# Two projections of a DiT block with 512 instead of 256 weight columns per matmul

## The chip, the cores and the metric

The kernel runs on one core of one Trainium2 chip. The metric is the device time of one execution in microseconds (us). A core has TensorE (PE: matmuls into PSUM), VectorE (DVE), ScalarE (ACT), GpSimd (POOL) and SyncE (SP, which here issues every DMA). Each engine works through its own list of instructions in order and waits on semaphores for the others.

## What is computed

One layer of a backbone for diffusion, on 1024 tokens with 1024 features, all in float32: a modulated RMSNorm, one input projection, two groups of heads side by side, an output projection, and a gated MLP with a 3x3 convolution. The part that matters here, cut down:

```python
def token_mixer(h, w_in, ...):
    z = h @ w_in
    zq, zf_f, zf_b, zi, zg, zu = jnp.split(z, ...)        # 512 columns each
    ...                                                   # q, k, v: forward and backward gated scans
    o = rms_norm(o_f + flip(o_b), g_norm) * jax.nn.silu(heads(zg))
    uf = zu.reshape(B, L, 4, 128)
    y_four = jnp.fft.fft2(uf, axes=(1, 3), norm='ortho').real
    return jnp.concatenate([o, y_four], axis=-1)
```

## The kernel before, in words

Matmuls are done in three products: a float32 operand is split into a high part `hi` (rounded to fp32r) and a low part `lo`, and `mm3` adds hi*hi, hi*lo and lo*hi into one PSUM block. A weight page is a tile of 128 x 1024. `wload` loads it raw into one of two buffers `wr`, ScalarE casts it to `hi` (L62), and VectorE subtracts to get `lo` (L63). By default `hi` and `lo` go into the pools `wh` and `wl`, which have two buffers each; the pool `pg` has 33 pages of the same size for everything else (the normed activations `hT` take 16 of them).

The program goes: `start` (norm, projection of `zi`), then four heads in turn (`head_gemm` does their projections with features on the partitions, `hgrn` the chunked scans on VectorE, ScalarE and TensorE), then `mod_part(0)`, `(2)`, `(1)` (modulation vectors: VectorE sums over weights that stream in, L219 and L221, TensorE transposes, L224), `fnet_proj`, `fnet`, `gate_proj`, `gate`, `mod_part(3)`, `out_proj`, and `ffn`. In `hgrn`, the scores stand at L74 (psm), then transposes (L545), products with v (L74), a chain of states on VectorE (L553) and the output products, which ScalarE evacuates at L564.

`fnet_proj` and `gate_proj` are the two projections with tokens on the partitions. Both call `proj_nat`: a slice of 128 tokens is the stationary operand, weight columns move. Before, it goes through two pieces of 256 columns; each piece has two pages (each with four blocks of 128 rows, 256 columns wide), used for all eight token slices, so the four pages of a projection pass through `wh` and `wl` two at a time. A block `psg` of PSUM holds four token slices. `fnet_proj` evacuates into U[0..3] (L596), `gate_proj` through a Silu into four tiles `zg` (L676).

`fnet` does the DFT over positions: VectorE adds and subtracts the U tiles (butterflies, L606 to L621), then for each of four channel groups TensorE multiplies with DFT tables, ScalarE evacuates (L643), TensorE multiplies again, VectorE combines (L662, L663), ScalarE casts the result (L666) and VectorE makes its low part (L667). `gate` scales the heads' outputs (L688), transposes them (L694) and splits them (L696, L697) for `out_proj`.

The order of instructions on each engine is not written out. A scheduler takes the instructions by their place in the program as far as their operands and a free buffer in their pool are there; `wload` has a higher priority from the first head on (`self.ahead`). So work that stands later in the program fills gaps of work that stands earlier, if a buffer for it is free.

Of the kernel before, what the change touches and what calls it, by code (L numbers as in the profile page):

```python
# [34 lines left out]
class Kern:  # L35
# [533 lines left out]
                                     accum_out=self.ssq[:, h * NT + n:h * NT + n + 1])  # L569


    def proj_nat(self, src, evac):

        for piece in range(2):
            ws = [self.wload(src[piece, i]) for i in range(2)]
            for half in range(2):
                pt = self.pst("g")
                for i in range(4):
                    n = 4 * half + i
                    t = slice(i * P, (i + 1) * P)  # L580
                    steps = []
                    for kt in range(NK):
                        q = slice((kt % 4) * 256, (kt % 4 + 1) * 256)
                        wh, wl = ws[kt // 4]
                        hi, lo = self.hT[kt][half]
                        steps.append(((hi[:, t], lo[:, t]), [(wh[:, q], wl[:, q])]))
                    self.mm3([pt[:, i * 256:(i + 1) * 256]], steps)
                evac(piece, half, pt)

    def fnet_proj(self):  # L590
        self.U = [self.pg(F32, "zt") for _ in range(4)]

        def evac(piece, half, pt):
            for j in range(2):
                u = self.U[2 * half + j].rearrange("p (n c) -> p n c", n=2)
                self.nc.scalar.copy(u[:, :, piece * 256:(piece + 1) * 256],  # L596
                                    pt[:, j * 512:(j + 1) * 512].rearrange("p (n c) -> p n c", n=2))
        self.proj_nat(self.I["wzu"], evac)

    def fnet(self):  # L600
        nc, V = self.nc, self.nc.vector
        U = self.U
        C = math.sqrt(0.5)
        s01, s23, d01, d23 = (self.pg() for _ in range(4))
        for o, a, b, op in ((s01, U[0], U[2], ADD), (s23, U[1], U[3], ADD), (d01, U[0], U[2], SUB), (d23, U[1], U[3], SUB)):
            V.tensor_tensor(o, a, b, op=op)  # L606
        lo, hi = slice(0, 512), slice(512, 1024)
        e02, o13, p02, p13 = (self.pg() for _ in range(4))
        V.tensor_tensor(e02, s01, s23, op=ADD)
        V.tensor_tensor(o13[:, lo], s01[:, lo], s23[:, lo], op=SUB)  # L610
        V.tensor_tensor(o13[:, hi], s23[:, hi], s01[:, hi], op=SUB)
        g04 = self.pg()
        V.tensor_tensor(g04[:, lo], e02[:, lo], e02[:, hi], op=ADD)
        V.tensor_tensor(g04[:, hi], e02[:, lo], e02[:, hi], op=SUB)
        V.tensor_tensor(p02[:, lo], d01[:, hi], d23[:, hi], op=SUB)
        V.tensor_tensor(p02[:, hi], d01[:, hi], d23[:, hi], op=ADD)
        g1, g3 = p13, self.pg()
# [1 line left out]
        V.scalar_tensor_tensor(g1[:, hi], p02[:, hi], -C, d23[:, lo], op0=MUL, op1=SUB)  # L619
        V.scalar_tensor_tensor(g3[:, lo], p02[:, lo], -C, d01[:, lo], op0=MUL, op1=ADD)  # L620
        V.scalar_tensor_tensor(g3[:, hi], p02[:, hi], -C, d23[:, lo], op0=MUL, op1=ADD)  # L621
        G = [(g04[:, lo], None), (g1[:, lo], g1[:, hi]), (o13[:, lo], o13[:, hi]), (g3[:, lo], g3[:, hi]), (g04[:, hi], None)]
        tw = [self.pg() for _ in range(3)]
        for i in range(3):
# [44 lines left out]


    def gate_proj(self):
        self.zg = {}

        def evac(piece, half, pt):
            z = self.zg[piece, half] = self.pg(F32, "zt")
            self.nc.scalar.activation(z, pt, AF.Silu)  # L676
        self.proj_nat(self.I["wzg"], evac)

    def gate(self):
        nc, V = self.nc, self.nc.vector  # L680
        r = self.rsqrt_mean(self.ssq, 32, 1.0 / P, "ro")
        gn = self.vec[:, V_HG:V_HG + 1]
        for h in range(NH):
            o = self.o[h]
            for n in range(NT):
                t = slice(n * P, (n + 1) * P)
                z = self.zg[h // 2, n // 4][:, (n % 4) * 256 + (h % 2) * P:(n % 4) * 256 + (h % 2 + 1) * P]
                V.scalar_tensor_tensor(o[:, t], o[:, t], r[:, h * NT + n:h * NT + n + 1], z, op0=MUL, op1=MUL)  # L688
            yh, yl = self.pg(F32R), self.pg(F32R)
            for half in range(2):  # L690
                pt = self.pst("m")
                for i in range(4):
                    n = 4 * half + i
                    nc.tensor.transpose(pt[:, i * P:(i + 1) * P], o[:, n * P:(n + 1) * P], self.ident)  # L694
                s = slice(half * 512, (half + 1) * 512)
                nc.scalar.activation(yh[:, s], pt, AF.Copy, scale=gn)  # L696
                V.scalar_tensor_tensor(yl[:, s], pt, gn, yh[:, s].bitcast(F32), op0=MUL, op1=SUB)  # L697
            self.y[h] = (yh, yl)
# [554 lines left out]
def lay_out(x, c, ctx, c_ctx, w_mod, b_mod, norm1, norm2, w_in, lb_fwd, lb_bwd,  # L1253
            hgrn_norm, w_out, w_up, w_dw, b_dw, w_down, norm_f):
    A = np.ascontiguousarray
    w_mod, w_in, w_out, w_up, w_down = w_mod[0], w_in[0], w_out[0], w_up[0], w_down[0]
    col = lambda v: np.asarray(v).reshape(-1, P).T
    vec = np.concatenate([
        col(b_mod[0]), col(norm1[0]), col(norm2[0]), col(norm_f), col(hgrn_norm[0]),
        col(lb_fwd), col(lb_bwd), col(b_dw[0]),  # L1260
        w_dw[0].reshape(9, NF, P).transpose(2, 1, 0).reshape(P, NF * 9),
        col(c[0]), col(c_ctx)], axis=1)
    assert vec.shape == (P, NV)
    rows = lambda w: w.reshape(NK, P, -1)
    win = rows(w_in)
    ctile = lambda i: win[:, :, i * P:(i + 1) * P].transpose(1, 0, 2).reshape(P, 1024)
    nat = lambda a: win[:, :, a:a + 512].reshape(2, 4, P, 2, 256).transpose(3, 0, 2, 1, 4).reshape(2, 2, P, 1024)
    out = {
        "xT": x[0].T.reshape(NK, P, L),
        "ctxT": ctx[0].T.reshape(2, 4, P, LC).transpose(0, 2, 1, 3).reshape(2, P, 1024),  # L1270
        "vec": vec,
        "wm1": w_mod[:, :2048].reshape(2, 4, P, 2, 8, P).transpose(4, 0, 2, 1, 3, 5).reshape(8, 2, P, 1024),
        "wm2": w_mod[:, 2048:].reshape(NK, P, 4, 1024).transpose(2, 0, 1, 3),
        "wT": np.stack([ctile(4 + i) for i in range(8)] + [ctile(i) for i in range(4)]),
        "wzi": win[:, :, 1536:2048].reshape(4, 2, P, 512).transpose(0, 2, 1, 3).reshape(4, P, 1024),
        "wzg": nat(2048),
        "wzu": nat(2560),
        "wo": rows(w_out).reshape(NK, P, NK, P).transpose(2, 1, 0, 3).reshape(NK, P, 1024),
        "wup": rows(w_up).reshape(NK, P, 2, NF, P).transpose(3, 2, 1, 0, 4).reshape(NF, 2, P, 1024),
        "wd": w_down.reshape(NF, P, D),  # L1280
    }
    out = {k: A(np.asarray(a, dtype=np.asarray(a).dtype)) for k, a in out.items()}
    out.update(shape_constants())
    return out
# [16 lines left out]
```

## Time and profile before

| | |
|---|---|
| time, median of 3 runs | 1234.57 us (1233.62 to 1239.16) |
| the profiled execution: its time, its span | 1235.95 us, 1234.2 us |
| TensorE busy | 1191.5 us, 97% of the span |
| VectorE, ScalarE, GpSimd busy | 913.7 us (74%), 559.3 us (45%), 201.7 us (16%) |
| DMA | 146.23 MB, mean 118 GB/s |
| TensorE's mean granted clock | 0.987 |

Times inside the execution are counted from the start of the span. TensorE's busy time is made of instructions that overlap in a pipeline, with modelled ends, so a busy share near 100% doesn't mean that it works at its peak. The granted clock is a share of full speed: 1.00 is 2.4 GHz and 0.50 is 1.2 GHz. In a chain of waits each piece is the work that the next one waited for.

### The profile page before, as it was taken

What the parts mean: (1) busy time and instruction counts of PE and PEld (TensorE: products, weight loads), DVE (VectorE), ACT (ScalarE), POOL (GpSimd) and SP (SyncE); (2) the same over time, 40 slices, a digit from 0 to 9 for tenths busy, and PEclk for the clock granted to TensorE, in tenths of its full rate; (3) what the DMA queues carried; (4) which work ended last, traced back from release to release, by engine and by line L of the source; (5) the groups of instructions that cost most, each with busy time, mean ns of one, the idle gap of its engine ahead of it and who ended that gap; (6) DMA issues with size and microseconds to landing.
All of it is one profiled execution on the core that took longest, in us unless ns stands there. A gap on an engine that the chain in (4) does not pass through costs nothing.

```text
span 1234.2 us, 15757 instructions
## 1 busy us (share of the span) xinstructions
PE 1191.5 (97%) x6120; PEld 996.5 (81%) x6120; DVE 913.7 (74%) x1173; ACT 559.3 (45%) x804; POOL 201.7 (16%) x124
## 2 busy tenths in 40 slices
PE   7999999999999999999989999999999999999997
PEld 4688888888998888888868888888888887887876
DVE  5761758585877457577989897888888888997683
ACT  5634545454431424364544444444354433335551
POOL 0000000000000000001336455364463400000000
PEclk9999999999999999999989999999999999999998
DMA  8631101010256037453122322222212438635642
GB/s 327 234 121 38 39 18 35 18 35 18 86 162 205 10 120 263 156 187 103 34 77 77 112 94 78 89 90 86 86 69 94 145 111 304 244 112 185 221 157 99
DMA packets 57867, 146.23 MB, mean 118 GB/s; under 512 B 5568, under 2 KB 5824, under 8 KB 57792
## 3 DMA queue, kind: packets, MB, share of 16 engines
q1 hardware_dynamic: 57792, 145.22, 34.1%
q8 instruction: 48, 0.79, 0.3%
q14 instruction: 27, 0.22, 0.1%
HBM read 125.27 MB, written 19.92 MB: 118 GB/s over the span
## 4 chain that ended last, share of the span: by engine, by line
PE 63%; DVE 14%; ACT 9%; DMA 8%; issue 5%; SPq 0%; POOL 0%; DVEq 0%; ACTq 0%; POOLq 0%
PE psm L859 27%; PE psm L74 16%; PE psg L74 14%; PE psm L1036 3%; DMA wr<-in_wd_dram 2%; DVE cv L930 2%; DVE wl L63 2%; DMA wm<-in_wm_dram 2%; DVE pg L451 1%; DMA pg<-gd 1%; ACT wh L62 1%; DMA wx<-gd 1%; ACT sq L568 1%; DVE sl L63 1%; PE psg L1036 1%
## 5 line engine op out<-in xcount | busy, mean ns | idle before, releaser
L930 DVE SCALAR_TENSOR_TENSOR cv<-psg,vec,cv 128x945 f32<-128x945 f32 (+2 forms) x176 | 213.8, 1219 | 26.9 <-ACT cv L922 23.1
L859 PE MATMUL psm<-pg,sh 128*128 128x512 f32 x640 | 199.1, 393 | 5.5 <-ACT sn L939 5.5
L62 ACT CAST wh<-wr 128x1024 fp32r<-128x1024 f32 x78 | 82.0, 1053 | 144.3 <-PE psg L74 39.7
L859 PEld LDWEIGHTS psm<-pg,sh 128*128 128x128 f32 x640 | 121.3, 190 | 31.6 <-ACT sn L939 6.3
L74 PE MATMUL psg<-pg,wh 128*128 128x512 f32 x472 | 134.8, 394 | 0.0
L63 DVE TENSOR_TENSOR wl<-wr,wh 128x1024 fp32r<-128x1024 f32 x78 | 96.5, 1238 | 41.2 <-ACT wh L62 40.8
L839 POOL TENSOR_TENSOR ws<-wx 128x512 f32<-128x512 f32 x20 | 27.9, 1394 | 601.8 <-DMA wx<-in_wup_dram 568.0
L859 PE MATMUL psm<-pg,sl 128*128 128x512 f32 x320 | 125.4, 392 | 0.0
L74 PEld LDWEIGHTS psg<-pg,wh 128*128 128x128 f32 x472 | 87.2, 188 | 16.8
L74 PE MATMUL psg<-wh,pg 128*128 128x256 f32 x512 | 99.0, 292 | 1.0 <-ACT wh L62 0.8
L859 PE MATMUL psm<-pg,wh 128*128 128x512 f32 x320 | 98.4, 389 | 0.0
L939 ACT ACTIVATE sn<-psm 128x512 f32<-128x512 f32 x80 | 47.6, 596 | 108.7 <-PE psm L859 108.7
L74 PEld LDWEIGHTS psg<-wh,pg 128*128 128x128 f32 x512 | 83.0, 197 | 1.6 <-ACT wh L62 1.4
L74 PE MATMUL psg<-pg,wl 128*128 128x512 f32 x236 | 79.1, 395 | 0.0
L74 PE MATMUL psg<-wl,pg 128*128 128x256 f32 x256 | 74.5, 292 | 4.6 <-DVE wl L63 4.6
L859 PEld LDWEIGHTS psm<-pg,sl 128*128 128x128 f32 x320 | 60.6, 190 | 12.7
L859 PEld LDWEIGHTS psm<-pg,wh 128*128 128x128 f32 x320 | 60.1, 188 | 12.4
L905 POOL TENSOR_TENSOR uu<-sn,sn 128x512 f32<-128x512 f32 x20 | 38.5, 1924 | 183.0 <-ACT sn L939 183.0
L859 PE MATMUL psm<-pg,wl 128*128 128x512 f32 x160 | 62.2, 389 | 0.0
L74 PE MATMUL psm<-pg,pg 128*128 128x128 f32 (+2 forms) x256 | 56.6, 348 | 5.0 <-DVE pg L506 4.7
L221 DVE SCALAR_TENSOR_TENSOR ma<-wm,silu_c,ma 128x512 f32<-128x512 f32 x56 | 41.9, 749 | 17.8 <-DMA wm<-in_wm_dram 17.2
L847 POOL TENSOR_TENSOR sl<-ws,sh 128x1024 fp32r<-128x1024 f32 x20 | 54.1, 2706 | 5.6 <-ACT sh L846 5.5
(368 smaller groups left out, 2590.3 us busy)
## 6 DMA issues: line engine op xcount, KB each, us to landing
wr<-in_wd_dram SPq DMA_DIRECT2D x35, 512.0 KB, 3.7
wm<-in_wm_dram SPq DMA_DIRECT2D x64, 256.0 KB, 3.0
wx<-in_wup_dram SPq DMA_DIRECT2D x22, 512.0 KB, 4.5
wr<-in_wup_dram SPq DMA_DIRECT2D x22, 512.0 KB, 3.6
gd<-cv SPq DMA_DIRECT2D x22, 512.0 KB, 2.6
pg<-gd SPq DMA_DIRECT2D x33, 256.0 KB, 4.9
ld<-in_wm_dram SPq DMA_DIRECT2D x16, 512.0 KB, 7.9
wr<-in_wo_dram SPq DMA_DIRECT2D x16, 512.0 KB, 3.6
```

Source lines behind the costliest of these rows:

```text
L62: self.nc.scalar.copy(hi, raw)
L63: self.nc.vector.tensor_tensor(lo, raw, hi.bitcast(F32), op=SUB)
L74: self.nc.tensor.matmul(out, lhsT, rhs, start=start, stop=stop)
L221: nc.vector.scalar_tensor_tensor(acc, w, s, acc, op0=MUL, op1=ADD)
L451: V.tensor_tensor_scan(flip(lf, d), flip(lf, d), self.mscan, 0.0, op0=ADD, op1=MUL)
L839: G.tensor_tensor(s31[:, hi], u[:, lo], u[:, hi], op=ADD)
L847: G.tensor_tensor(S31[1], s31, S31[0].bitcast(F32), op=SUB)
L859: self.nc.tensor.matmul(out, w[a][:, q], B[kt // 2][b][:, t], start=(first and kt == 0 and j == 0), stop=(kt == 3 and j == 2), skip_group_ ...
L905: self.nc.gpsimd.tensor_tensor(u[:, h1], s7, s5, op=SUB)
L930: V.scalar_tensor_tensor(c3[:, ro, co], a3[:, ri, ci], w9((dr + 1) * 3 + dc + 1), c3[:, ro, co], op0=MUL, op1=ADD)
L939: self.nc.scalar.mul(dst, src, c)
L1036: nc.tensor.matmul(pts[j], W[a][:, w], G[b][:, t], start=first and p == 0 and i == 0 and m == 0, stop=p == n - 1 and m == 2, skip_group_ch ...
```

## The change

`proj_nat` now loads all four pages of a projection ahead of its matmuls. A page has two blocks of 128 rows, 512 columns wide; `lay_out` stores `wzu` and `wzg` that way. The loop goes through the eight token slices, with all 512 columns in one matmul, and a PSUM block holds two token slices. The pages' pools are given by the caller: `fnet_proj` puts the first two in `wh`/`wl` and the last two in `pg`, `gate_proj` the first two in `pg` and the last two in `wh`/`wl`. Each PSUM block is evacuated at once into one U or `zg` tile, which now holds two token slices with all columns; `gate` indexes them so. In `fnet` some tiles are made later and some names are dropped earlier. The lines of the profile move by one or two from `fnet` on.

```diff
--- before.py
+++ after.py
@@ -569,49 +569,47 @@
                                      accum_out=self.ssq[:, h * NT + n:h * NT + n + 1])
 
 
-    def proj_nat(self, src, evac):
-
-        for piece in range(2):
-            ws = [self.wload(src[piece, i]) for i in range(2)]
-            for half in range(2):
+    def proj_nat(self, src, tags, evac):
+
+        ws = [self.wload(src[i], *tags[i // 2]) for i in range(4)]
+        for n in range(NT):
+            if n % 2 == 0:
                 pt = self.pst("g")
-                for i in range(4):
-                    n = 4 * half + i
-                    t = slice(i * P, (i + 1) * P)
-                    steps = []
-                    for kt in range(NK):
-                        q = slice((kt % 4) * 256, (kt % 4 + 1) * 256)
-                        wh, wl = ws[kt // 4]
-                        hi, lo = self.hT[kt][half]
-                        steps.append(((hi[:, t], lo[:, t]), [(wh[:, q], wl[:, q])]))
-                    self.mm3([pt[:, i * 256:(i + 1) * 256]], steps)
-                evac(piece, half, pt)
+            t = slice((n % 4) * P, (n % 4 + 1) * P)
+            steps = []
+            for kt in range(NK):
+                q = slice((kt % 2) * 512, (kt % 2 + 1) * 512)
+                wh, wl = ws[kt // 2]
+                hi, lo = self.hT[kt][n // 4]
+                steps.append(((hi[:, t], lo[:, t]), [(wh[:, q], wl[:, q])]))
+            self.mm3([pt[:, (n % 2) * 512:(n % 2 + 1) * 512]], steps)
+            if n % 2:
+                evac(n // 2, pt)
 
     def fnet_proj(self):
         self.U = [self.pg(F32, "zt") for _ in range(4)]
-
-        def evac(piece, half, pt):
-            for j in range(2):
-                u = self.U[2 * half + j].rearrange("p (n c) -> p n c", n=2)
-                self.nc.scalar.copy(u[:, :, piece * 256:(piece + 1) * 256],
-                                    pt[:, j * 512:(j + 1) * 512].rearrange("p (n c) -> p n c", n=2))
-        self.proj_nat(self.I["wzu"], evac)
+        self.proj_nat(self.I["wzu"], (("wh", "wl"), ("pg", "pg")), lambda i, pt: self.nc.scalar.copy(self.U[i], pt))
 
     def fnet(self):
         nc, V = self.nc, self.nc.vector
         U = self.U
         C = math.sqrt(0.5)
         s01, s23, d01, d23 = (self.pg() for _ in range(4))
-        for o, a, b, op in ((s01, U[0], U[2], ADD), (s23, U[1], U[3], ADD), (d01, U[0], U[2], SUB), (d23, U[1], U[3], SUB)):
-            V.tensor_tensor(o, a, b, op=op)
+        V.tensor_tensor(s01, U[0], U[2], op=ADD)
+        V.tensor_tensor(s23, U[1], U[3], op=ADD)
+        V.tensor_tensor(d01, U[0], U[2], op=SUB)
+        V.tensor_tensor(d23, U[1], U[3], op=SUB)
         lo, hi = slice(0, 512), slice(512, 1024)
-        e02, o13, p02, p13 = (self.pg() for _ in range(4))
+        e02, o13 = self.pg(), self.pg()
         V.tensor_tensor(e02, s01, s23, op=ADD)
         V.tensor_tensor(o13[:, lo], s01[:, lo], s23[:, lo], op=SUB)
         V.tensor_tensor(o13[:, hi], s23[:, hi], s01[:, hi], op=SUB)
+        del s01, s23
         g04 = self.pg()
         V.tensor_tensor(g04[:, lo], e02[:, lo], e02[:, hi], op=ADD)
         V.tensor_tensor(g04[:, hi], e02[:, lo], e02[:, hi], op=SUB)
+        del e02
+        p02, p13 = self.pg(), self.pg()
         V.tensor_tensor(p02[:, lo], d01[:, hi], d23[:, hi], op=SUB)
         V.tensor_tensor(p02[:, hi], d01[:, hi], d23[:, hi], op=ADD)
         g1, g3 = p13, self.pg()
@@ -619,6 +617,7 @@
         V.scalar_tensor_tensor(g1[:, hi], p02[:, hi], -C, d23[:, lo], op0=MUL, op1=SUB)
         V.scalar_tensor_tensor(g3[:, lo], p02[:, lo], -C, d01[:, lo], op0=MUL, op1=ADD)
         V.scalar_tensor_tensor(g3[:, hi], p02[:, hi], -C, d23[:, lo], op0=MUL, op1=ADD)
+        del p02, d01, d23
         G = [(g04[:, lo], None), (g1[:, lo], g1[:, hi]), (o13[:, lo], o13[:, hi]), (g3[:, lo], g3[:, hi]), (g04[:, hi], None)]
         tw = [self.pg() for _ in range(3)]
         for i in range(3):
@@ -669,12 +668,12 @@
 
 
     def gate_proj(self):
-        self.zg = {}
-
-        def evac(piece, half, pt):
-            z = self.zg[piece, half] = self.pg(F32, "zt")
-            self.nc.scalar.activation(z, pt, AF.Silu)
-        self.proj_nat(self.I["wzg"], evac)
+        self.zg = []
+
+        def evac(i, pt):
+            self.zg.append(self.pg(F32, "zt"))
+            self.nc.scalar.activation(self.zg[i], pt, AF.Silu)
+        self.proj_nat(self.I["wzg"], (("pg", "pg"), ("wh", "wl")), evac)
 
     def gate(self):
         nc, V = self.nc, self.nc.vector
@@ -684,7 +683,7 @@
             o = self.o[h]
             for n in range(NT):
                 t = slice(n * P, (n + 1) * P)
-                z = self.zg[h // 2, n // 4][:, (n % 4) * 256 + (h % 2) * P:(n % 4) * 256 + (h % 2 + 1) * P]
+                z = self.zg[n // 2][:, (n % 2) * 512 + h * P:(n % 2) * 512 + (h + 1) * P]
                 V.scalar_tensor_tensor(o[:, t], o[:, t], r[:, h * NT + n:h * NT + n + 1], z, op0=MUL, op1=MUL)
             yh, yl = self.pg(F32R), self.pg(F32R)
             for half in range(2):
@@ -1264,7 +1263,7 @@
     rows = lambda w: w.reshape(NK, P, -1)
     win = rows(w_in)
     ctile = lambda i: win[:, :, i * P:(i + 1) * P].transpose(1, 0, 2).reshape(P, 1024)
-    nat = lambda a: win[:, :, a:a + 512].reshape(2, 4, P, 2, 256).transpose(3, 0, 2, 1, 4).reshape(2, 2, P, 1024)
+    nat = lambda a: win[:, :, a:a + 512].reshape(4, 2, P, 512).transpose(0, 2, 1, 3).reshape(4, P, 1024)
     out = {
         "xT": x[0].T.reshape(NK, P, L),
         "ctxT": ctx[0].T.reshape(2, 4, P, LC).transpose(0, 2, 1, 3).reshape(2, P, 1024),
@@ -1272,7 +1271,7 @@
         "wm1": w_mod[:, :2048].reshape(2, 4, P, 2, 8, P).transpose(4, 0, 2, 1, 3, 5).reshape(8, 2, P, 1024),
         "wm2": w_mod[:, 2048:].reshape(NK, P, 4, 1024).transpose(2, 0, 1, 3),
         "wT": np.stack([ctile(4 + i) for i in range(8)] + [ctile(i) for i in range(4)]),
-        "wzi": win[:, :, 1536:2048].reshape(4, 2, P, 512).transpose(0, 2, 1, 3).reshape(4, P, 1024),
+        "wzi": nat(1536),
         "wzg": nat(2048),
         "wzu": nat(2560),
         "wo": rows(w_out).reshape(NK, P, NK, P).transpose(2, 1, 0, 3).reshape(NK, P, 1024),
```

How this moves instructions: first TensorE in the last head, from its first transposes on (`psm_2731` holds the first transposed block of keys, `psm_2737` the product with v behind it, `psg_3147` the second PSUM block of `fnet_proj`). Before:

```order
L545 MATMUL psm_2731<-ident,pg_2636 128x128 x4
L74 MATMUL psg_3147<-wl_3045,pg_613 128x256
L74 MATMUL psg_3147<-wh_3044,pg_614 128x256
L74 MATMUL psg_3147<-wh_3044,pg_613 128x256
L74 MATMUL psg_3147<-wl_3045,pg_613 128x256
L74 MATMUL psg_3147<-wh_3044,pg_614 128x256
L74 MATMUL psg_3147<-wh_3044,pg_659 128x256
L74 MATMUL psm_2737<-pg_628,k_2730 128x128 x4
L545 MATMUL psm_2746<-ident,pg_2636 128x128 x3
```

Now, from the last score product (`psm_2712`) on:

```order
L74 MATMUL psm_2712<-k_2607,k_2606 128x128 x4
L224 MATMUL psc_2888<-ident,ma_2863 128x128 x3
L545 MATMUL psm_2731<-ident,pg_2636 128x128 x4
L74 MATMUL psm_2737<-pg_628,k_2730 128x128 x4
L545 MATMUL psm_2746<-ident,pg_2636 128x128 x3
L74 MATMUL psm_2751<-pg_628,k_2730 128x128 x3
L545 MATMUL psm_2758<-ident,pg_2719 128x128 x4
```

The projection's matmuls no longer stand between the head's products; those with the pages in `pg` come behind the head.

Second, TensorE at the end of `fnet_proj`. Before, its last PSUM block (`psg_3357`) is followed by the first block of `gate_proj` (`psg_3629`):

```order
L74 MATMUL psg_3357<-wh_3254,pg_659 128x256
L74 MATMUL psg_3357<-wl_3255,pg_659 128x256
L74 MATMUL psg_3357<-wh_3254,pg_660 128x256
L74 MATMUL psg_3629<-wh_3619,pg_244 128x256
L74 MATMUL psg_3629<-wl_3620,pg_244 128x256
L74 MATMUL psg_3629<-wh_3619,pg_245 128x256
```

Now its last block (`psg_3210`) is followed by the first products of the DFT (`psm_3293`, `psm_3298`; the tables are `pg_3285` and `pg_3286`):

```order
L74 MATMUL psg_3210<-pg_3056,pg_659 128x512
L74 MATMUL psg_3210<-pg_3057,pg_659 128x512
L74 MATMUL psg_3210<-pg_3056,pg_660 128x512
L74 MATMUL psm_3293<-pg_3285,pg_3273 128x256
L74 MATMUL psm_3293<-pg_3285,pg_3277 128x256 x2
L74 MATMUL psm_3298<-pg_3286,pg_3269 128x256 x2
```

All matmuls of `gate_proj` have moved behind the DFT's last product.

Third, ScalarE at the end of `fnet`. Before, the cast of the fourth DFT result (`pg_3600`) stands between the evacuations of `gate_proj`, ahead of the casts of that projection's third and fourth page:

```order
L676 ACTIVATE zt_3726<-psg_3629 128x1024
L666 CAST pg_3600<-zt_3610 128x8x128
L62 CAST wh_3829<-wr_3827 128x1024
L62 CAST wh_3835<-wr_3833 128x1024
L676 ACTIVATE zt_3825<-psg_3728 128x1024
```

Now all four pages of `gate_proj`, the two in `pg` first, are cast behind the fourth DFT result (`pg_3404`):

```order
L665 CAST pg_3404<-zt_3414 128x8x128
L62 CAST pg_3423<-wr_3421 128x1024
L62 CAST pg_3429<-wr_3427 128x1024
L62 CAST wh_3435<-wr_3433 128x1024
L62 CAST wh_3441<-wr_3439 128x1024
```

The first cast for `gate_proj` has moved from ahead of the butterflies to behind the DFT.

## Rows read from the trace of the kernel before

**Rows 1.** The page, part 1: TensorE's busy time, share of the span and instructions.

```profile
PE 1191.5 (97%) x6120; PEld 996.5 (81%) x6120; DVE 913.7 (74%) x1173; ACT 559.3 (45%) x804; POOL 201.7 (16%) x124
```

**Rows 2.** The page, part 5: instructions | busy us, mean ns | idle before.

```profile
L62 ACT CAST wh<-wr 128x1024 fp32r<-128x1024 f32 x78 | 82.0, 1053 | 144.3 <-PE psg L74 39.7
...
L74 PE MATMUL psg<-pg,wh 128*128 128x512 f32 x472 | 134.8, 394 | 0.0
L63 DVE TENSOR_TENSOR wl<-wr,wh 128x1024 fp32r<-128x1024 f32 x78 | 96.5, 1238 | 41.2 <-ACT wh L62 40.8
...
L74 PE MATMUL psg<-wh,pg 128*128 128x256 f32 x512 | 99.0, 292 | 1.0 <-ACT wh L62 0.8
```

**Rows 3.** Chain of waits, 280 to 650 us: start us, us, what.

```profile
351.26 5.37 PE psm L74 x48
...
394.03 0.44 PE psc L224 x4
394.46 13.91 PE psg L74 x116
...
481.47 5.23 PE psm L74 x23
...
594.84 5.44 PE psg L74 x24
```

**Rows 4.** Timeline of TensorE, 70 to 94 us: start us, us, instructions.

```profile
73.07 20.89 PE L74 MATMUL psg<-pg,pg 128*128 128x512 f32 x90
```

**Rows 5.** Timeline of TensorE, 326 to 350 us; in brackets, idle before and releaser.

```profile
330.54 1.16 PE L74 MATMUL psm<-pg,pg 128*128 128x128 f32 x8 [1.45 <-DVE pg L506]
...
341.63 0.63 PE L545 MATMUL psm<-ident,pg 128*128 128x128 f32 x4
```

**Rows 6.** Stretches: us, TensorE busy (count), granted clock, DMA share, GB/s.

```profile
387.80:389.70 1.90, 0.00 (x0) 1.00 0.32 122
390.30:393.60 3.30, 3.30 (x18) 0.50 0.66 199
394.00:396.00 2.00, 2.00 (x20) 1.00 0.98 383
635.70:640.70 5.00, 0.00 (x0) 0.87 0.61 215
640.80:646.20 5.40, 5.40 (x13) 0.50 0.29 110
646.30:648.00 1.70, 1.70 (x9) 1.00 0.00 0
```

**Rows 7.** Timeline of VectorE, 280 to 480 us.

```profile
395.11 1.22 DVE L606 TENSOR_TENSOR pg<-zt,zt 128x1024 f32<-128x1024 f32 x1
...
403.94 0.68 DVE L619 SCALAR_TENSOR_TENSOR pg<-pg,pg 128x512 f32<-128x512 f32 x1
...
427.09 0.69 DVE L662 TENSOR_TENSOR zt<-psm,wm 128x512 f32<-128x512 f32 x1 [0.92 <-PE psm L74]
...
430.42 2.11 DVE L667 TENSOR_TENSOR pg<-zt,pg 128x1024 fp32r<-128x1024 f32 x1 [2.17 <-ACT pg L666]
433.44 0.69 DVE L662 TENSOR_TENSOR zt<-psm,wm 128x512 f32<-128x512 f32 x1 [0.91 <-PE psm L74]
```

**Rows 8.** Timeline of ScalarE, 280 to 480 us.

```profile
356.65 0.59 ACT L564 COPY pg<-psm 128x512 f32<-128x512 f32 x1 [1.65 <-PE psm L74]
```

**Rows 9.** DMA issues: count, size, median us to landing.

```profile
wr<-in_wzg_dram SPq DMA_DIRECT2D x4, 512.0 KB, 3.8
...
pg<-in_dft_dram SPq DMA_DIRECT2D x3, 512.0 KB, 6.1
```

**Rows 10.** Chain of waits, 404 to 470 us.

```profile
408.37 1.30 PE psm L74 x6
...
441.77 24.53 PE psg L74 x191
466.30 1.09 PE psm L694 x10
```

## The prediction

> **What bounds the kernel now.** I read the page's busy times first. TensorE is busy for 97% of the span [rows 1], so the question is what happens to TensorE's time; but the projections must not be priced by their busy column. There a 128x256 matmul has a mean of 292 ns and a 128x512 one of 394 ns [rows 2], which are times from start to end of instructions that overlap. The chain of waits gives the spacing: 116 narrow ones in 13.91 us, so 119.9 ns each, and 24 wide ones in 5.44 us, so 226.7 ns each [rows 3]. The form that this change uses (token slice stationary, 512 weight columns moving) is in the kernel already: 90 recorded in 20.89 us, 232 ns at most [rows 4]. So two narrow ones cost 239.8 ns and a wide one 226.7 ns: 13 ns won per pair.
>
> Then I read the stretch from the last head to the output projection in order of time, for who waits for whom. TensorE hardly stands still there, because the projections' matmuls are the filler in everything else. They fill the last head, while VectorE and ScalarE work: TensorE waits 1.45 us ahead of the scores [rows 5], and the last products form an unbroken 5.37 us [rows 3]. They also run beside VectorE's butterflies: the 116 above are gate matmuls, and the DFT follows them without a wait [rows 3, 10].
>
> The third thing is the granted clock [rows 6]. TensorE had no work from 387.8 to 389.7, and from 390.3 to 393.6 the clock is 0.50, 1.2 GHz: 1.7 us lost. After 5 us without work (635.7 to 640.7) it is 0.50 for 5.4 us of work: 2.7 us lost. I charge 1.7 us for each new gap, with 0 and 2.7 as bounds.
>
> The Trainium skill, TensorE: Matmul & The Clock Gate, HAM oscillation, says that gaps in which TensorE waits put the next stretch on the slow clock, which speaks against a change that opens gaps; rows 6 agree.
>
> **The change, leg by leg.** I walk TensorE's markers; order comes from the lists of instructions, every time from the trace. 384 wide matmuls (87.1 us) replace 768 narrow ones (92.1 us): 5 us less streaming. What counts is where they stand.
>
> *Leg 1, the last head.* Ahead of the first score product stood 106 narrow matmuls (12.7 us); now 24 wide ones (5.4 us), because pages 2 and 3 of the weights come later. TensorE runs dry 7.3 us earlier, but the scores wait for VectorE until 330.54 anyway [rows 5], so this costs a cold start only: midway between the two losses, 2.2 us. Among the head's transposes and products stood 59 narrow matmuls (7.1 us), now none. Most of them filled waits for ScalarE's copies. Between the first transpose (341.63) and the first output product (351.26) [rows 3, 5] I count 12 of them (1.4 us) beyond those waits, which is won; a second cold stretch behind the stand ahead of the transposes, 1.7 us, takes it back. Leg 1 ends at 356.6 + 2.5 = 359.1. Bounds: -1.4 (no cold clock) and +6.7 (a third cold stretch in the output products, 2.7 us each, less the 1.4).
>
> *Leg 2, the first projection.* 168 of its 192 wide matmuls are left. Two pool pages are cast only behind the head's evacuations in ScalarE's order: evacuation 0.59 [rows 8], cast 1.05, VectorE's split 1.24 [rows 2]. So all but two matmuls start 2.9 us behind leg 1, at 362.0. Then 166 x 0.2267 = 37.6, three groups of modulation transposes at 0.44 [rows 3] = 1.3, cold clock 1.7: 402.6. Before, it ended at 387.8 [rows 6], since 165 of its 384 narrow matmuls (19.8 us) had been filler. The modulation vectors (VectorE and its loads) had their last transposes at 394.0 [rows 3]; the new list reaches these at about 393, so they are hidden, and if late cost up to 2 us. Four evacuations of 128x1024 instead of eight of 128x512 hide under the next block; only the last shows.
>
> *Leg 3, the butterflies.* Before, TensorE had gate matmuls while VectorE worked. Now the first DFT matmul stands directly behind the last projection matmul. It waits for the last evacuation (0.1 + 1.05, taken from the cast of the same size [rows 2]) and for VectorE from the second butterfly to the end of the one that the second DFT product needs: 395.11 to 404.62, 9.5 us [rows 7]. 402.6 + 1.15 + 9.5 = 413.2, with TensorE without work for 10.6 us. The DFT's three tables are loaded in this time too, but land 6.1 us behind their issue [rows 9], so ahead of that.
>
> *Leg 4, the DFT.* From 408.37 [rows 3, 10] to VectorE's 433.44 [rows 7] is 25.1 us, four rounds of 6.35, led by a chain over all three engines; the 14 narrow matmuls between fill waits for ScalarE, so leaving them out wins nothing. Cold start 1.7. It ends at 413.2 + 25.1 + 1.7 = 440.0.
>
> *Leg 5, the gate projection.* Before, 232 of its 384 narrow matmuls were left at 433.44, and the last ended at 466.30 [rows 10]. Now all 192 wide ones (43.5 us) are left, and their first pages are pool pages, cast behind the DFT's last cast in ScalarE's order. From VectorE's marker: its last DFT split begins 3.33 later and takes 2.11 (430.42 against 427.09 [rows 7]), the first page's split 1.24: matmuls run from 6.6 on. 22 of them use pages 0 and 1: 5.0 + 1.7 cold. Pages 2 and 3 need the raw buffers that these splits free: at 6.6 and 7.8, load 3.8 [rows 9], cast 1.05, split 1.24, so ready at 12.7 and 13.9, about when the 22 are done (13.3). Then 170 x 0.2267 = 38.5. The end is 440.0 + 6.6 + 6.7 + 38.5 = 491.8, 25.5 us later than 466.3.
>
> *Leg 6, the tail to the output projection's third block* took 15.2 us (466.30 to 481.47 [rows 3, 10]). The lists have the same eight scalings, eight transposed half heads and 48 matmuls behind the last gate matmul; I charge nothing, plus or minus 1. What follows keeps its order on TensorE and is bound by it, so the shift stays. POOL has no part in this stretch; on SP's queue each weight load still stands behind the split that frees its buffer.
>
> Shifts at the markers: 2.5, 14.8, 4.8 (the DFT's start), 6.6, 25.5. The profiled execution took 1235.95 us, 1.4 more than the median of the runs shown, 1234.57; 1234.57 + 25.5 = 1260.1. Lower end: leg 1 at -1.4 and no cold clock in legs 2, 4 and 5 (-3.9 - 5.1): +16.5, 1251. Upper end: leg 1 at +6.7, 2.7 for each cold start, the vectors 2 us late (+4.2 + 3.0 + 2): +34.7, 1269.
>
> **The rivals.** Half a per cent, 6.2 us, is about what a measurement of this kernel can tell from no change.
> - *No cold clock*, and an earlier end of the head: 1251 (1248 to 1254). For it: the 1.45 us wait [rows 5] is followed by products at the usual pace. Against: 2 us without work already cost 1.7 [rows 6], and the gaps here are of 3 to 10.
> - *Cold through the head, and late vectors*: 1269 (1266 to 1273). For it: without filler the head's products leave TensorE short waits all along.
> - *Faster: the wide matmuls of the new form stream closer than in rows 3.* 166 + 192 = 358 of them lie on the path, so each nanosecond of spacing is 0.36 us, and below 226.7 - 25.5 / 0.358 = 155 ns the lost cover is paid for. Taken by the busy column (2 x 292 against 394) one would expect 73 us less; at 130 ns the time is 1226. Against it: the same form takes 232 ns at most and hardly less [rows 4], at full clock.
> - *No difference*: the gaps would have to close, which needs the pool pages' casts ahead of the DFT; ScalarE's list has them behind it. That the change doesn't do what it says is excluded by TensorE's list, which holds 384 matmuls of 512 columns.
>
> The Trainium skill, TensorE: Matmul & The Clock Gate, Back-to-back issue gap, gives about 131 ns for sustained 512-column matmuls; with it one would estimate 34 us less than my sum, 1226. The 226.7 ns of rows 3 differ, and decide.
>
> **How the numbers follow.** My forecast (1254 to 1266) 0.56; no cold clock 0.15; cold and late 0.21; faster 0.05; no difference 0.03. The likeliest gives 1260. The range takes both bounds with 3 us for the tail and the spread of runs: 1248 to 1273; it leaves out faster and no difference, 0.08, and some of both ends. Faster by over 0.5%: 0.05; within: 0.03; slower: 0.92.
>
> **What would show it.** Right: 384 projection matmuls with a mean near 393 ns at a spacing of 227; TensorE without work for about 10 us ahead of the DFT, ended by VectorE's butterflies, and for about 5 us behind it, ended by a split; a clock of 0.50 behind both; the last gate matmul near 492, the output projection's third block near 507. Wrong: a spacing well below 227, gate matmuls ahead of the DFT, or a last gate matmul before 475.

## The result, and the profile after

The changed kernel takes 1267.32 us (median of 4 runs, 1264.79 to 1272.32), against 1234.66 us before (1233.62 to 1239.16), measured beside it: ratio 1.0262, 95% interval 1.0221 to 1.0304. The direction and the range held; the time lies 7 us above the forecast of 1260.1 and 1.3 us outside what the prediction gave its likeliest case (1254 to 1266). It is inside what it gave its second rival (cold through the head, and late vectors: 1266 to 1273).

The profiled execution took 1266.04 us, with a span of 1264.3. In it everything ahead of the change lies 2.6 us earlier than in the one before, where the instructions are still the same: the scan of the first head starts at 121.46 against 124.08, the scores of the last head at 327.95 against 330.54 [rows 5]. This is spread between executions (121.3 to 124.1 in the kernels of this document), so the markers are compared from the scores' start.

| marker | before | after | shift from the scores' start | forecast |
|---|---|---|---|---|
| first transposes of the last head | 341.63 | 341.26 | +2.2 | +2.2 |
| first output product | 351.26 | 353.56 | +4.9 | |
| end of the head | 356.6 | 360.5 | +6.5 | +2.5 |
| end of `fnet_proj` | 387.8 | 406.4 | +21.2 | +14.8 |
| start of the DFT (after: its second product) | 408.37 | 416.41 | +10.6 | +4.8 |
| VectorE's marker in the DFT | 433.44 | 443.53 | +12.7 | +6.6 |
| end of the gate matmuls | 466.30 | 496.04 | +32.3 | +25.5 |
| third block of the output projection | 481.47 | 511.20 | +32.3 | +25.5 |

TensorE's work, from the page's part 1 (busy us, share of the span, instructions), for [rows 1]:

```profile
PE 1196.7 (95%) x5736; PEld 980.8 (78%) x5736; DVE 914.6 (72%) x1173; ACT 559.8 (44%) x800; POOL 201.9 (16%) x124
```

There are 384 instructions fewer, and the span is 30 us longer. The chain of waits of the changed kernel (start us, us, what) answers to [rows 3, 7, 10]:

```profile
327.95 8.76 PE psm L74 x56
...
341.26 0.64 PE psm L545 x4
...
363.40 11.88 PE psg L74 x44
...
396.43 10.01 PE psg L74 x44
406.46 1.02 ACT zt L591
407.50 1.23 DVE pg L599
...
415.75 0.61 DVE pg L616
416.41 5.33 PE psm L74 x12
...
443.53 0.69 DVE zt L661
...
448.86 1.22 DVE pg L63
450.13 45.91 PE psg L74 x190
```

Two things are to be seen. 44 wide matmuls take 10.01 us, so 227.5 ns each: the spacing of [rows 3] holds, and nothing streams closer. And at two places the chain runs over the other engines while TensorE has next to nothing to do: from 406.5 to 416.4 for the evacuation and the butterflies, and from 443.5 to 450.1 for the DFT's end and the gate pages; behind that stand all gate matmuls in one piece. What TensorE waited for between 318 and 500 us (engine, line, waited for: us in total, times, longest):

```profile
PE psm L74 <- DVE pg L506: 9.0, 1, 9.0
PE psm L74 <- DVE pg L609: 7.6, 1, 7.6
PE psg L74 <- ACT pg L62: 5.0, 2, 3.8
PE psm L545 <- DVE pg L528: 3.0, 1, 3.0
PE psm L74 <- ACT k L546: 2.5, 4, 0.7
PE psg L74 <- DVE pg L63: 2.2, 2, 1.7
PE psc L224 <- DVE ma L221: 1.7, 2, 1.2
...
PE psm L74 <- DVE pg L616: 1.2, 1, 1.2
```

L506 holds the scores (before: 1.45 us [rows 5]), L609 and L616 are butterflies for the first two products of the DFT (the first product runs at 414.00; the lines are the changed kernel's, which among the butterflies lie two to eight below those before), and the L62 and L63 rows are cast and split of the pool pages. The clock, by stretches (us, TensorE busy, granted clock, DMA share, GB/s), answers to [rows 6]:

```profile
319.00:328.00 9.00, 0.05 (x1) 0.69 0.27 87
328.00:333.00 5.00, 5.00 (x25) 0.53 0.48 161
333.00:341.00 8.00, 5.30 (x46) 1.00 0.10 33
341.00:347.00 6.00, 4.45 (x21) 0.66 0.09 30
347.00:353.50 6.50, 5.26 (x23) 0.50 0.28 94
353.50:357.00 3.50, 3.50 (x20) 0.56 0.36 126
357.00:361.00 4.00, 3.95 (x36) 1.00 0.63 217
...
363.40:367.40 4.00, 4.00 (x11) 0.57 0.86 250
...
416.40:421.40 5.00, 4.99 (x12) 0.50 0.00 0
...
443.50:450.10 6.60, 1.10 (x6) 0.90 0.36 119
450.10:456.00 5.90, 5.87 (x15) 0.54 0.72 239
```

Behind each stand the clock falls to 0.50, as forecast (a row's mean takes in its edges; the five stretches here are those behind the scores' wait, the transposes' wait, the restart, the butterflies and the gate pages). What was not forecast is how long it stays there in the head: from about 343 to 356.6, through the products with v, the transposes between them and half of the output products.

### The profile page after: what moved, and what is told of

Its sections match the earlier page's. It is cut to its first block, busy times and chain, and to the rows that moved or that the text cites. A ratio compares the mean times of both kernels' runs of the same rounds, so it can differ in the third digit from the quotient of the medians.

```text
span 1264.3 us, 14978 instructions
## 1 busy us (share of the span) xinstructions
PE 1196.7 (95%) x5736; PEld 980.8 (78%) x5736; DVE 914.6 (72%) x1173; ACT 559.8 (44%) x800; POOL 201.9 (16%) x124
## 4 chain that ended last, share of the span: by engine, by line
PE 65%; DVE 14%; ACT 9%; DMA 7%; issue 4%; SPq 0%; DVEq 0%; ACTq 0%
PE psm L858 30%; PE psm L74 15%; PE psg L74 13%; PE psm L1035 4%; DVE wl L63 2%; DMA wm<-in_wm_dram 1%; DMA wr<-in_wd_dram 1%; DVE pg L451 1%; DMA pg<-gd 1%; ACT wh L62 1%; DMA wx<-gd 1%; DVE sl L63 1%; PE psg L1035 1%; ACT L444 1%; ACT L445 1%
## 5 line engine op out<-in xcount | busy, mean ns | idle before, releaser
L858 PEld LDWEIGHTS psm<-pg,sh 128*128 128x128 f32 x640 | 121.3, 190 | 31.6 <-ACT sn L938 6.2
L62 ACT CAST wh<-wr 128x1024 fp32r<-128x1024 f32 x74 | 77.9, 1052 | 138.9 <-PE psm L74 36.5
L63 DVE TENSOR_TENSOR wl<-wr,wh 128x1024 fp32r<-128x1024 f32 x74 | 91.8, 1240 | 40.3 <-ACT wh L62 39.7
L74 PE MATMUL psg<-pg,pg 128*128 128x512 f32 x384 | 98.2, 407 | 8.4 <-ACT pg L62 5.0
L74 PEld LDWEIGHTS psg<-pg,pg 128*128 128x128 f32 x384 | 73.7, 196 | 27.3 <-ACT pg L62 5.5
L74 PE MATMUL psm<-pg,pg 128*128 128x128 f32 (+2 forms) x256 | 61.4, 371 | 22.6 <-DVE pg L506 12.2
L74 PEld LDWEIGHTS psm<-pg,pg 128*128 128x128 f32 x256 | 44.0, 206 | 33.8 <-DVE pg L506 13.9
```

The lines of the kernel that those rows point to most:

```text
L62: self.nc.scalar.copy(hi, raw)
L63: self.nc.vector.tensor_tensor(lo, raw, hi.bitcast(F32), op=SUB)
L74: self.nc.tensor.matmul(out, lhsT, rhs, start=start, stop=stop)
L858: self.nc.tensor.matmul(out, w[a][:, q], B[kt // 2][b][:, t], start=(first and kt == 0 and j == 0), stop=(kt == 3 and j == 2), skip_group_ ...
```

## The experiments

Two theories stood at the start. *Lost cover*: the wide matmuls are no slower than the narrow ones, but the two pages in the common pool come too late to fill the head, the butterflies and the DFT. The rival: the width itself, with its larger evacuations and blocks that need all four pages, is what costs.

| kernel | time, us | ratio to before, 95% interval |
|---|---|---|
| the change | 1267.32 | 1.0262 (1.0221 to 1.0304) |
| both projections' pages asked for early | 1228.13 | 0.9931 (0.9909 to 0.9952) |
| only `fnet_proj`'s | 1249.03 | 1.0095 (1.0073 to 1.0118) |
| only `gate_proj`'s | 1244.88 | 1.0066 (1.0044 to 1.0087) |
| the change with 256 columns | 1280.81 | 1.0357 (1.0335 to 1.0379) |
| both early, 256 columns | 1231.64 | 0.9968 (0.9950 to 0.9985) |
| the change, head kept warm | 1261.05 | 1.0207 (1.0176 to 1.0237) |
| both early, four `wm` buffers | 1227.70 | 0.9939 (0.9922 to 0.9956) |
| that, gate in pieces ahead of the groups | 1225.57 | 0.9919 (0.9891 to 0.9948) |
| that, pieces behind the groups | 1224.77 | 0.9895 (0.9862 to 0.9927) |
| both early, beside the one above | 1227.90 | 0.9922 (0.9897 to 0.9948) |

### The same pages, asked for earlier

Why do the pool pages come late? In the changed kernel's instruction lists, counted from first write to last read, never more than 28 of the pool's 33 pages are in use from the last head's scans through the DFT. So it doesn't lack pages. But `fnet_proj`'s first pool page is cast only behind the evacuations into `o`, the last tile that the head takes from the pool, and `gate_proj`'s first only behind the last tile that the DFT takes. That looks as if this pool hands out its buffers in the order in which the program first uses its tiles, whatever the priority of the request. If so, it is enough to write the requests earlier. Nothing else is touched in this edit: the loop over `wload` becomes a function `pages`, and the two calls move.

```diff
             self.ahead = True
+            if h == NH - 1:
+                self.wu = self.pages(self.I["wzu"], (("wh", "wl"), ("pg", "pg")))
             self.hgrn(h, g)
...
         self.fnet_proj()
+        self.wg = self.pages(self.I["wzg"], (("pg", "pg"), ("wh", "wl")))
         self.fnet()
```

> The change as it is (512 columns, the same pages in the same pools, the same evacuations), but the four weight pages of each projection are asked for earlier in the program: fnet_proj's ahead of the last head's scans, gate_proj's ahead of the butterflies. Lost-cover theory (the change costs because the two pages in the common pool get their buffers only in program order, behind every pool tile of the stage that they should fill, so TensorE has no filler): TensorE's list now has 105 wide matmuls up to the head's end (82.5 pairs before the change), 177 up to the DFT (178.5), 96 behind it (116). The loss goes altogether and 384 x 13 ns = 5 us of streaming and the 1.45 us wait ahead of the scores are won: 1228 us, 1224 to 1238. Rival, the width itself (wide matmuls, single evacuations of 128x1024, or a gate block that needs all pages) costs: 1255 or more. Rival, half and half: 1245.

Measured: 1228.13 us, the time that the lost-cover theory gave. In its chain of waits the gate matmuls end 8.5 us earlier than before the change (457.82 against 466.30 [rows 10]); 1.45 of these it has ahead of any difference, since its first head's scan starts at 122.63 against 124.08:

```profile
402.42 5.23 PE psg L74 x23
407.65 1.29 PE psm L74 x6
...
435.74 22.08 PE psg L74 x96
457.82 1.09 PE psm L695 x10
```

Its DFT begins directly behind gate matmuls again, and 96 wide ones are left behind it in place of 192. What TensorE still waits for, from 300 to 530 us:

```profile
PE psc L224 <- DVE ma L221: 3.4, 3, 1.4
PE psg L74 <- ACT zt L677: 2.7, 1, 2.7
PE psm L74 <- DVE pg L506: 2.0, 1, 2.0
```

The 7.6, 5.0 and 3.0 us of the changed kernel are gone. The 1.45 us ahead of the scores, which the expectation counted as won, are not: that wait is 2.0 us here, so that the time was met without this term. The same kernel, measured again beside the last one below, gave 0.9922.

Each half was then moved alone.

> Only fnet_proj's pages are asked for early, gate_proj's as in the change. Lost-cover theory: legs 1 and 2 are repaired, legs 3 and 5 are not. The first projection ends near 386, the DFT starts at about 404 to 405 because VectorE's vectors and butterflies set it (395.1 + 9.5 before the change), the marker is 430 to 431, and all 192 gate matmuls follow with a start 6.6 us and pages 13 us behind: last gate matmul near 483, 16 us later than before: 1251 us, 1246 to 1256. Rival, the loss sits in the head and the first projection alone: 1235 or less. Rival, width: no better than the change, 1262 or more.

Measured: 1249.03 us. Each marker came about 5 us earlier than written (425.5 and 477.8 in place of 430 to 431 and 483), the time 2 us earlier. TensorE's waits show the price of the gap that is left: 12.0 us for the modulation vectors, 10.8 of them at once, at a place where no gate matmul stands in its list, and behind the DFT 3.8 and 1.7 us for the gate pages, as in the change.

> Only gate_proj's pages are asked for early, fnet_proj's as in the change. Lost-cover theory: the head and the first projection lose as in the change (first projection's end about 16 us later than before), but about 60 gate matmuls (14 us) now run while VectorE does the butterflies, and 122 (27.7 us) are left behind the DFT against 232 narrow ones (27.8 us) before: 8 to 12 us slower than before, 1245 us, 1241 to 1250. Together with the run with fnet_proj's pages early it should add up: the two repairs (about 16 and 22 us) and the whole loss of 33 plus the 5 to 6 us of gain. Rival, the loss sits behind the DFT alone: 1236 or less. Rival, width: 1262 or more.

Measured: 1244.88 us, as the theory gave. The head keeps its 9.0 and 3.0 us of waits, but in the chain of waits 100 matmuls now lead to the DFT, and 122 are left behind it:

```profile
397.69 22.70 PE psg L74 x100
420.39 1.29 PE psm L74 x6
...
445.79 27.71 PE psg L74 x122
```

By the ratios the two repairs are worth 0.0167 and 0.0196 alone, or 21 and 24 us, and 0.0331 together, 41 us: nearly a sum. That shows the cause of the loss: it is the place at which the pages are asked for, and the same 512 columns stand in all these kernels. The rule by which the pool hands out buffers is read from the lists; that moving the request moves the casts, and the time, is shown.

### The price of the width

Two wide-against-narrow pairs, one without the cover and one with it. The edit is the same in both: two accumulations of 256 columns, one behind the other.

```diff
-                steps.append(((hi[:, t], lo[:, t]), [(wh[:, q], wl[:, q])]))
-            self.mm3([pt[:, (n % 2) * 512:(n % 2 + 1) * 512]], steps)
+                steps.append(((hi[:, t], lo[:, t]), wh[:, q], wl[:, q]))
+            for c in range(2):
+                c = slice(c * 256, c * 256 + 256)
+                self.mm3([pt[:, (n % 2) * 512:(n % 2 + 1) * 512][:, c]],
+                         [(a, [(h[:, c], l[:, c])]) for a, h, l in steps])
```

> The change's four pages, pools, order of pages and evacuations, but each wide matmul is done as two of 256 columns (two accumulations one after the other for each token slice), so 768 narrow matmuls again. Lost-cover theory: nothing of the cover comes back, and the streaming gets 13 ns longer for each of about 358 pairs on the path: 4.7 us more than the change, 1272 us, 1266 to 1278; spacing 120 ns. Rival, the 512-column form is what costs: back to 1235 to 1245. Rival, wide matmuls stream much closer than 227 ns: 1285 or more.

Measured: 1280.81 us, above the range given (1266 to 1278). The rival falls, since going back to 256 columns is slower, not faster. But it is 12 us slower than the change by the ratios, where 4.7 were expected. The trace shows why: in this form the first two pages feed fewer us of work. In the head 24 narrow matmuls stand (2.9 us) where 24 wide ones (5.4) stood, so 12 pairs more (2.9 us) are left for behind it. From the scores' start (328.42) to the end of the first projection (413.97) it takes 7.0 us longer than in the change: those 2.9, 2.2 of streaming, and 1.6 more of waits for the vectors (3.3 us in place of 1.7) make 6.7 of them. And behind the DFT the load of the third page lies bare on the path.

```profile
456.18 1.23 DVE pg L63
457.42 5.07 DMA wr<-in_wzg_dram
462.51 1.05 ACT wh L62
463.59 1.24 DVE wl L63
464.87 44.84 PE psg L74 x358
```

In the change the same load is hidden behind the 22 wide matmuls on pages 0 and 1. So this pair doesn't measure the width alone, since it loses more cover. The next one keeps the cover in both.

> The kernel of the first experiment (both projections' pages asked for early), with each wide matmul done as two of 256 columns: the price of the width alone, with the cover kept. Lost-cover theory with a spacing of 227 against 2 x 120 ns: TensorE is full nearly everywhere in this stretch, so 384 x 13 ns = 5.0 us more than the first experiment: 1233 us, 1230 to 1237. Rival, the width is worth more than its streaming (fewer weight loads to wait for, closer order): 1240 or more. Rival, the width is worth nothing: 1228.

Measured: 1231.64 us, 0.0037 or 4.6 us more than the wide form by the ratios, though the two intervals touch. Its gate matmuls behind the DFT, in the chain of waits:

```profile
436.48 23.30 PE psg L74 x192
```

That is 121 ns each, and 23.30 us where 96 wide ones took 22.08: 13 ns a pair, as forecast. With cover the width is worth about its streaming; the rival of 1240 or more falls, while the times alone would hardly tell 4.6 us from nothing.

### The cold clock in the head

> The change as it is, with 54 extra 128x512 matmuls on hT (results thrown away) in the last head: 40 in the 9 us without work ahead of the scores, 14 in the wait ahead of the transposes. Cold-clock theory for the part of leg 1 that was forecast too small: at full clock the way from the scores' start to the first output product takes about 20 us instead of 25.6, and the output products 1.5 us less; the granted clock is 1.00 from the scores to the head's end. Of the 5 to 6 us some is lost again to the modulation vectors, which set the first projection's pace: 1262 us, 1259 to 1264. Rival, the head's chain over ScalarE and VectorE without filler is what costs, at any clock: 1266 or more, and 25 us between the two markers.

```diff
+    def warm(self, n):
+        pw, (a, _) = self.pst("m"), self.hT[0][0]
+        for _ in range(n):
+            self.mm(pw, a[:, :P], a)
...
         sT = self.pg()
+        if h == NH - 1:
+            self.warm(40)
```

(The second call, `self.warm(14)`, stands ahead of the transposes.) Measured: 1261.05 us, 1 below the expected. From the scores' start to the first output product it takes 20.9 us (329.20 to 350.10) in place of 25.6. The timeline of TensorE in the head:

```profile
329.20 1.13 PE L74 MATMUL psm<-pg,pg 128*128 128x128 f32 x8 [1.39 <-DVE pg L511]
...
341.85 0.60 PE L554 MATMUL psm<-ident,pg 128*128 128x128 f32 x4
...
347.27 1.16 PE L74 MATMUL psm<-pg,k 128*128 128x128 f32 x8 [0.68 <-ACT k L555]
...
349.32 0.94 PE L74 MATMUL psm<-pg,k 128*128 128x128 f32 x6 [0.57 <-ACT k L555]
350.10 0.39 PE L74 MATMUL psm<-pg,pg 128*128 128x128 f32 x2
...
351.54 0.49 PE L74 MATMUL psm<-pg,pg 128*128 128x128 f32 x2 [0.84 <-DVE k L562]
```

In the change the first output product stands at:

```profile
353.56 0.64 PE L74 MATMUL psm<-pg,pg 128*128 128x128 f32 x2
```

The waits for ScalarE's copies in the warm run are nearly those of the change (2.3 us in all against 2.5), but the products between them go at full speed:

```profile
343.00:352.00 9.00, 6.18 (x46) 1.00 0.45 135
```

The way from the first transposes to the first output product is 8.3 us here, against 12.3 in the change and 9.63 before [rows 3, 5]. So the 1.4 us that the prediction saved by leaving out filler beyond the waits are real at full clock, and the cold clock turned them into a loss. The output products, expected 1.5 us faster, are only 0.3 faster (6.6 us against 7.0), since at full clock they wait 0.84 us for VectorE's states (L562 here). From the scores' start the head's end comes 5.0 us earlier than in the change, and the first projection's end 4.5: the vectors take back less than 1. The rest of the loss stays, since the later gaps are as they were.

### Towards a faster kernel

The early kernel still waited for the vectors and behind the DFT. First, four buffers `wm` in place of three:

> The first experiment's kernel, with four instead of three buffers for the streamed weights of the modulation vectors. In the first experiment TensorE waited 3.4 us, three times, for these vectors, whose chain alternates between VectorE and the loads. If the loads' buffers limit that chain: 1 to 3 us less than the first experiment, 1226 us, 1224 to 1228. Rival, the DMA engines or VectorE's other work limit it: no change, 1228 to 1230.

Measured: 1227.70 us, no change. TensorE's wait for the vectors went from 3.4 to 2.7 us only; the buffers don't limit that chain, and what does stays open. Then the gate projection was written in four pieces among the DFT's groups:

```diff
+        self.gate_proj(0)
         for g in range(4):
...
             self.y[NH + g] = (yh, yl)
+            if g < 3:
+                self.gate_proj(g + 1)
```

> As the run with four buffers, and the gate projection is written in four pieces of two token slices between the DFT's channel groups, so that its evacuations' tiles and instructions stand between those of the DFT. TensorE then has gate matmuls in the DFT's waits (3.4 us without work in the first experiment, 2.7 of it behind the DFT), and 96 matmuls no longer stand behind it. Theory: 3 us less than the run with four buffers: 1223 us, 1219 to 1226. Rival, the last evacuation, the scalings and the transposes behind it are uncovered now: 1226 to 1232.

Measured: 1225.57 us. The early kernel's stretch of the DFT (us, TensorE busy, clock, DMA share, GB/s):

```profile
402.00:436.00 34.00, 30.61 (x130) 1.00 0.15 45
```

The same stretch with the pieces, where TensorE is busy throughout:

```profile
402.00:436.00 34.00, 34.00 (x148) 1.00 0.02 10
```

But among its waits is a new one, for the last DFT split, which no gate matmul covers any more:

```profile
PE psg L74 <- DVE pg L669: 1.6, 1, 1.6
```

So each piece was put behind its group, the last one behind the last group:

```diff
-        self.gate_proj(0)
         for g in range(4):
...
-            if g < 3:
-                self.gate_proj(g + 1)
+            self.gate_proj(g)
```

> As the run with the gate projection in pieces, but each piece stands behind its channel group, the last one behind the last group. In that run TensorE waited 1.6 us for the last DFT split, with no gate matmul left; now 46 gate matmuls (10.4 us) stand there. Theory: 1 to 2 us less than it: 1223 us against 1235 before, ratio 0.990, 0.987 to 0.993. Rival, the last gate evacuation and the scalings behind it come uncovered instead: ratio 0.993 or more.

> The first experiment's kernel again, beside the run with the pieces behind their groups, on the same chip: ratio 0.993, 0.991 to 0.996. If the pieces win anything, this one is 3 to 5 us slower than that; if they don't, within 1.5 us of it.

Measured side by side: 1224.77 us against 1227.90, ratios 0.9895 and 0.9922. The 1.6 us wait is gone, and the pieces are likely worth some 3 us, but the intervals overlap. All the versions of this section beat both kernels.

## Why the prediction was right, and where it fell short

- **Spacing and filler: right.** Wide matmuls stand 227 to 230 ns apart, a pair of narrow ones 243, and the busy column would have misled, as it did before [rows 2]. The step on which all hangs, that the matmuls' place decides and not their width, is what the early pages show: the same matmuls cost 33 us in one place and win 8 in the other.
- **Leg 1: the cold clock was mis-sized, +6.5 in place of +2.5.** The first cold stretch came out as forecast (+2.2 at the first transposes). The step that failed is "a second cold stretch ..., 1.7 us, takes it back". It measured 4.0 (12.3 against 8.3 at full clock), and the output products took 1.6 more than before: 2.2 + 4.0 - 1.4 + 1.6 is 6.4 of the 6.5. That the clock cost the 4.0 is shown by the warm run. That it cost the 1.6 is read from its row only (3.5 us at 0.56): the warm run got back 0.3 of it, and a wait for VectorE took the rest. 1.7 was read off a stretch without waits [rows 6]; here the products have short waits between them and the clock didn't come back. The bound of +6.7 held this case, but by another path, a third, separate stretch in the output products; that the time stayed inside the range is luck to that extent.
- **Leg 2: +14.7 in place of +12.3.** The restart, 2.9 us behind the head, and the cold stretch (4.0 us at a mean of 0.57, so 1.7) came as forecast. The vectors did not stay hidden: TensorE waited 1.7 us for them in this leg, inside the "up to 2" of the prediction. It had left their last transposes at 394.0, which is 63.5 us behind the scores' start; they came at 395.8, 67.9 behind it. From the transposes at the head's end to these, 37.6 us passed before (from 356.45) and 35.5 now (from 360.35), so it is likely that the late head of leg 1 made the vectors late too; no run shows that by itself.
- **Leg 3: right** (-10.6 against -10.0). 10.0 us pass between the last projection matmul (406.4) and the DFT's second product, with 7.6 and 1.2 us of waits for butterflies in them. Forecast were 10.6: the sum ran to the end of the second butterfly that this product needs, but it starts when the first one (L616) is done, one of 0.6 us earlier.
- **Leg 4: right** (+2.1 against +1.8). The clock was at 0.50 for 5.0 us of work, so 2.5 us lost where 1.7 was put. Its "four rounds of 6.35" are one of 6.03 and three of 6.35; the 25.1 that the sum uses is right.
- **Leg 5: right** (+19.6 against +18.9). The first pool page's split came 6.6 us behind the marker, as reckoned. The cold stretch was 2.7 us (5.9 at 0.54) where 1.7 was put. Pages 2 and 3 cost nothing.
- **Leg 6: right.** 511.20 - 496.04 = 15.2 us, as before.

The misses of legs 1 and 2, 4.0 and 2.4 us, make nearly all of the 6.8 between forecast and measured shift. Both belong to the rival to which the prediction gave 0.21, so what came is that rival and not the likeliest case. The rivals of no cold clock and of closer streaming are excluded by the rows above. The case of no difference asked for the gate pages' casts ahead of the DFT. The run that did only that closed this gap and still lost 8 us, so the condition was half of what it needs: the other half are `fnet_proj`'s pages.

The Trainium skill, TensorE: Matmul & The Clock Gate, A second HAM failure mode: psum-queue depth-cycling, says that frequent short idles between groups of matmuls can make the clock go back and forth between its two levels. The rows here do not bear that out for waits of 0.5 to 0.7 us: in the change they go with 0.50, but behind a stand of 3.0 us, and in the warm run the same waits go with 1.00.

## What to carry to other kernels

Before a matmul is made wider, ask whether it was filler: what it saves is the difference in spacing times its count (here 5 us), and what it can lose is every wait that it had covered (here 33 us net). Where tiles share a pool with the stage that they should fill, look in the instruction lists for the place of their first write, not only at the free pages; to write the request earlier in the program may be all that is needed. When you charge a cold clock, look at what follows the gap: dense work came back to full speed after 1.7 to 2.7 us lost, and the one stretch of sparse work here stayed slow until it became dense (343 to 356.6 us).

## What was not expected of the hardware

- Here the clock followed what went before, and not the present waits alone. In the change the products with v, between waits of 0.5 to 0.7 us, had 0.50 (347.0 to 353.5 us), with the clock down since the stand of 3.0 us ahead of the transposes; in the warm run, where filler stood in place of that stand, the same products between the same waits had 1.00 throughout (343 to 352 us).
- 54 matmuls whose results are thrown away, 12 us at their spacing, made the kernel faster by some 6 us (1267.32 to 1261.05; the intervals of the two ratios just overlap, but the 5.0 us at the head's end are in the traces).
